# Six pairs of a triangular inverse merged in one pass, and norm weights loaded first

## The chip, the cores and the metric

The kernel runs on one core of a Trainium2 chip. The metric is the device time of one execution in microseconds (us). Engine names are those of the profile: PE is the matmul engine TensorE, DVE is VectorE, ACT is ScalarE, POOL is GpSimd, SP is SyncE, whose queue issues nearly all transfers.

## The reference

One layer of a decoder trunk: 256 tokens of width 2048, 256 memory tokens. The token mixer is a gated DeltaNet with 24 value heads of width 128 (two heads share one key and query head, which makes 12 pairs). Beside it runs a cross-attention with 4 heads. Both read columns of one input projection; the result is gated by SiLU and goes through one output projection.

The part that the change touches is the chunked delta rule. For each head and chunk a unit lower triangular system is solved:

```python
kk = jnp.einsum("bhncd,bhnjd->bhncj", k, k)
m = jnp.where(strict, beta[..., :, None] * kk * decay, 0.0) + jnp.eye(C, dtype=f32)
rhs = jnp.concatenate([v * beta[..., None], k * (beta * jnp.exp(gc))[..., None]], axis=-1)
sol = lax.linalg.triangular_solve(m, rhs, left_side=True, lower=True, unit_diagonal=True)
```

The kernel uses chunks of 128 tokens, so it has 12 pairs x 2 heads x 2 chunks = 48 matrices of 128x128 to invert, four to a pair.

## The kernel before

**Main stream.** Weights come in 275 tiles of 512 KB. SP issues their loads into five buffers `st`; ACT rounds each to `wt` (the high part) and DVE subtracts to get the low part; PE multiplies. Two forms of stream products exist: `pa` (a 512-column and a 256-column product for each of 16 blocks) and `pb` (three 512-column products for each block). `PLAN` is the list of weight tiles in the order in which they are used: memory values and keys, gates, cross-attention queries, key tiles, SiLU gates (`Z`), query and value tiles, output projection (`o`).

**What sets the order.** The kernel is written by a planner. It keeps an estimate `now` of the time on PE, advanced by `mm` for each product, and estimates of when ACT and DVE are free. Work beside the stream is written as generators that say with `yield` how long to wait, and with `until` on what; `step_side` runs those that are due between two stream products. `pe_soon` waits until the copies issued so far should be done. Instructions issued before `now` = 45 us, or put through `keep_in_program_order`, stay in the written order; the rest is ordered by a scheduler with times of its own, so a written run of small products can be cut by stream products. Every engine executes its own queue strictly in order: an instruction that waits holds all behind it.

**Start.** `first_loads` issues on ACT's queue the first half of the first memory tile `mst`, then the small table `prm` (norm weights), then the second half. `mem_prep` on DVE multiplies `mst` by a column of `prm` into `mkt`, high and low part; a stream product needs `mkt` and `wt`. `WARM` small products on zeros run before. In `gates`, an ACT instruction reads `prm` into `nA`, and a DVE instruction reads `nA`.

**Inverse.** Pairs 0 to 5 are group 0, pairs 6 to 11 are group 1. `inverse(g)` waits for the six pairs' matrices (`gram`), gets the 32x32 diagonal blocks through DRAM, inverts them on DVE column by column, and writes them to DRAM in two layouts, `dX` (natural) and `dY` (transposed). Then, for each two pairs (three times in a group), POOL clears `XN` and two `Y`, SP issues 6 transfers into `XN` and 8 into `Y`, and `merge` puts the blocks together:

```python
for s_ in range(4):
    for e, f in ef:
        mm(a1[at(e, f), s_, :], n2[e][f + 32 : f + 64, s_, f : f + 32], ys[e][f + 32 : f + 64, s_, f + 32 : f + 64],
           start=True, stop=True)
yield 0.2
se.copy(a, a1)
yield from pe_soon()
```

Four such runs follow each other, each needing the copies of the one before: 16 products of 32x32 (`pm<-Y,dec`), 24 of 32x32 (`pm<-Am,XN` and `pm<-XN,Am`), 8 of 64x64 (`pm<-Y,dec`) and 8 of 64x64 (`pm<-A,XN`). ACT copies the results back (`Am`, `XN`, `Y`, `A`). One fp32 product is two records of the trace. The result `Y` of a pair is what `delta` multiplies with.

**Delta.** `delta(p)` runs for pairs 0 to 11 in order (`pkq`, `pvt`, `pU`, `pO`, `pqs` products), each after the pair's `Y`, its value tiles and the delta before. `split_y` transposes its result (`pyT`) for the output projection, whose last weight tile of each column block needs pair 11.

Of the kernel before, what the change touches and what calls it, by code (L numbers as in the profile page):

```python
# [21 lines left out]
NB = 2  # L22
# [9 lines left out]


LOOK = 2
WARM = 7
XPACE = 3.0
HOP = 0.25
PINNED = 45.0
SLACK = 0.7
POLL = 0.3  # L40
CALM = 1.6
INV_CALM = 1.2
GATE_CALM = 1.6
LATE_DECAY = ("q", 3)
# [37 lines left out]
def hybrid_kernel(ctx: ExitStack, tc: tile.TileContext, x, xT, memT, W, prm_d, cst_d, out):  # L82
# [3 lines left out]
    def pin(ins):  # L86

        return tc.keep_in_program_order(ins) if PINNED is None or now[0] < PINNED else ins
# [57 lines left out]
    cp = ctx.enter_context(tc.tile_pool(name="cp", bufs=1))  # L146
    stp = ctx.enter_context(tc.tile_pool(name="stp", bufs=5))
    wp = ctx.enter_context(tc.tile_pool(name="wp", bufs=4))
    s2p = ctx.enter_context(tc.tile_pool(name="s2p", bufs=66))
    smp = ctx.enter_context(tc.tile_pool(name="smp", bufs=3))  # L150
    ps = ctx.enter_context(tc.tile_pool(name="ps", bufs=1, space=PSUM))
    dp = ctx.enter_context(tc.tile_pool(name="dp", bufs=1, space=DRAM))
# [1 line left out]
    def S2(name, shape, dt=F32):  # L154
        return s2p.tile([128] + list(shape), dt, name=name, tag="s2")

    def SM(name, shape, bufs=3, dt=F32):
        n = 1
        for d in shape:
            n *= d  # L160
        if n > 128:
            return smp.tile([128] + list(shape), dt, name=name, tag="s1k", bufs=12)
        if n > 16:
            return smp.tile([128] + list(shape), dt, name=name, tag="s512", bufs=3)
        return smp.tile([128] + list(shape), dt, name=name, tag=name, bufs=bufs)
# [20 lines left out]
    def bank(tag, name):  # L186
        yield from until(lambda: spare(tag))
        return PS(tag, name)
# [8 lines left out]
    def mm(o_, lhsT, rhs, start, stop):  # L197
        n = width(rhs)
        if rhs.dtype == F32:
            now[0] += {32: 0.015, 64: 0.038}.get(rhs.shape[0], max(0.19, 4 * n / 2400.0))  # L200
        else:
            now[0] += max(0.092, n / 2400.0 + 0.017)
        te.matmul(o_, lhsT, rhs, start=start, stop=stop)
# [96 lines left out]

    def first_loads():

        mst[0] = S2("mst", [512])
        for a in range(2):
            w = slice(a * 256, (a + 1) * 256)
            pin(nc.scalar.dma_start(mst[0][:, w], memT[0][:, w]))
            if a == 0:
                pin(nc.scalar.dma_start(prm[:, 0:P_CW], prm_d[:, 0:P_CW]))

    def wnext():  # L310
        while wpos[0] < len(PLAN) and free:
# [303 lines left out]
    def gates(pt):  # L615
# [14 lines left out]
        ve.tensor_scalar(out=gn[rbeta], in0=ab[rbeta], scalar1=-1.0, scalar2=80.0, op0=ALU.mult, op1=ALU.min)  # L630
        ve.scalar_tensor_tensor(out=gn[ra], in0=gx[ra], scalar=-1.0, in1=gx[ra], op0=ALU.mult, op1=ALU.min)
        yield
        se.activation(nA[ra, 0:1], prm[ra, P_AL : P_AL + 1], AF.Exp)
        se.activation(gu[ra], gn[ra], AF.Exp)
        se.activation(gu[rbeta], gn[rbeta], AF.Exp)
        yield
# [256 lines left out]
    def inverse(g):  # L893
        yield from until(lambda: all(p in grams for p in range(6 * g, 6 * g + 6)))
        yield 0.5
        nn = [S2("inN", [16, 32])[0:96] for _ in range(2)]
        xt = [S2("inXT", [16, 32])[0:96] for _ in range(2)]
        for f in range(2):
            sd.dma_start(nn[f], diag(dN[g])[:, 16 * f : 16 * f + 16])
        for f in range(2):  # L900
            po.memset(xt[f], 0.0)
        yield
        for f in range(2):
            po.memset(xt[f].rearrange("s c r -> s (c r)")[:, 16 * f : 512 : 33], 1.0)
        yield
        for i in range(1, 32):
            yield from calm(INV_CALM)
            work = []
            for f in range(2):
                w, j0 = min(16, i - 16 * f), 16 * f  # L910
                if w > 0:
                    tm = S2("inT", [16 * 32])[0:96]
                    work.append((f, w, j0, tm[:, 0 : w * (i - j0)].rearrange("s (c j) -> s c j", c=w)))
            for f, w, j0, tv in work:
                ve.tensor_tensor(out=tv, in0=xt[f][:, 0:w, j0:i],
                                 in1=nn[i // 16][:, i % 16, j0:i].unsqueeze(1).to_broadcast([96, w, i - j0]), op=ALU.mult)
            for f, w, j0, tv in work:
                ve.tensor_reduce(out=xt[f][:, 0:w, i], in_=tv, axis=AX.X, op=ALU.add)
            if len(work) == 1:
                ve.run(0.25)  # L920
        yield
        xn = nn
        for f in range(2):
            for e in range(2):
                ve.tensor_copy(xn[e][:, :, 16 * f : 16 * f + 16], xt[f][:, :, 16 * e : 16 * e + 16].rearrange("s c r -> s r c"))
        yield
        for f in range(2):
            sd.dma_start(dY[g][:, 16 * f : 16 * f + 16], xt[f])
        for f in range(2):
            sd.dma_start(dX[g][:, 16 * f : 16 * f + 16], xn[f])  # L930
        yield
        nat = dX[g].rearrange("(s k) r c -> k r s c", k=4)
        tsp = dY[g].rearrange("(s k) r c -> k r s c", k=4)
        for q in range(3):
            xs = S2("XN", [8, 64])
            ys = [S2("Y", [4, C]) for _ in range(2)]
            for t in [xs] + ys:
                po.memset(t, 0.0)
            yield
            for e in range(2):  # L940
                for k, r0, c0 in ((0, 64 * e, 0), (1, 64 * e + 32, 32), (2, 96 - 64 * e, 0)):
                    sd.dma_start(xs[r0 : r0 + 32, 4 * e : 4 * e + 4, c0 : c0 + 32],
                                 nat[k][:, 8 * q + 4 * e : 8 * q + 4 * e + 4])
            for p2 in range(2):
                s0 = 8 * q + 4 * p2
                for k in range(4):
                    b = slice(32 * k, 32 * k + 32)
                    sd.dma_start(ys[p2][b, :, b], tsp[k][:, s0 : s0 + 4])
            yield
            yield from merge(6 * g + 2 * q, xs, ys)  # L950

    def merge(p0, xs, ys):

        n2 = [N2[p0 + e].rearrange("r b h c -> r (b h) c") for e in range(2)]
        ef = [(e, f) for e in range(2) for f in (0, 64)]

        def at(e, f):

            r = 64 * e if f == 0 else 96 - 64 * e
            return slice(r, r + 32)

        pm = yield from bank("m", "pm")
        a1, y12, x21 = [pm[:, w * 128 : w * 128 + 128].rearrange("r (s c) -> r s c", s=4) for w in range(3)]
        a = SM("Am", [4, 32])
        for s_ in range(4):
            for e, f in ef:
                mm(a1[at(e, f), s_, :], n2[e][f + 32 : f + 64, s_, f : f + 32], ys[e][f + 32 : f + 64, s_, f + 32 : f + 64],
                   start=True, stop=True)  # L970
        yield 0.2
        se.copy(a, a1)
        yield from pe_soon()
        for s_ in range(4):
            for e, f in ef:
                r = at(e, f)
                mm(y12[r, s_, :], xs[r, 4 * e + s_, 0:32], a[r, s_, :], start=True, stop=True)
            for e in range(2):
                r = at(e, 0)
                mm(x21[r, s_, :], a[r, s_, :], xs[r, 4 * e + s_, 0:32], start=True, stop=True)  # L980
        yield 0.2
        for e in range(2):
            se.copy(xs[64 * e + 32 : 64 * e + 64, 4 * e : 4 * e + 4, 0:32], x21[at(e, 0)])
        for e, f in ef:
            se.copy(ys[e][f : f + 32, :, f + 32 : f + 64], y12[at(e, f)])
        give(pm, se.end)
        yield from pe_soon()
        pm2 = yield from bank("m", "pm2")
        a2, yab = [pm2[:, w * 256 : w * 256 + 256].rearrange("r (s c) -> r s c", s=4) for w in range(2)]
        A2 = SM("A2", [4, 64])  # L990
        for s_ in range(4):
            for e in range(2):
                mm(a2[64 * e : 64 * e + 64, s_, :], n2[e][64:128, s_, 0:64], ys[e][64:128, s_, 64:128], start=True, stop=True)
        yield 0.2
        se.copy(A2, a2)
        yield from pe_soon()
        for s_ in range(4):
            for e in range(2):
                r = slice(64 * e, 64 * e + 64)
                mm(yab[r, s_, :], xs[r, 4 * e + s_, :], A2[r, s_, :], start=True, stop=True)  # L1000
        yield 0.2
        for e in range(2):
            se.copy(ys[e][0:64, :, 64:128], yab[64 * e : 64 * e + 64])
        give(pm2, se.end)
        yield from pe_soon()
        for e in range(2):
            Y[p0 + e], N2[p0 + e] = ys[e].rearrange("r (b h) c -> r b h c", b=NB), None


    yhi, ylo = [None] * 16, [None] * 16  # L1010
# [75 lines left out]
    def delta(p):  # L1086
# [61 lines left out]
        yield from pe_soon()  # L1148
        for h in range(2):
            mm(B[:, 256 + h * C : 256 + (h + 1) * C], y[:, 1, h, :], vs[:, 1, h, :], start=True, stop=True)  # L1150
        A = yield from bank("A", "pO1")
        exact(A[:, 256:512], (kch[:, 1, :], kcl[:, 1, :]), (uh, ul), start=True, stop=True)
        yield 0.2
# [83 lines left out]
    first_loads()  # L1237
    spawn(mem_stats(), 8.0)
    spawn(tok_prep(), 8.0)
    spawn(inverse(0))  # L1240
    spawn(inverse(1))
    for hd in range(4):
# [90 lines left out]
```

## Time and profile before

| | |
|---|---|
| median of 3 runs | 879.3 us (878.26 to 879.44) |
| profiled execution | 878.1 us, span of its instructions 876.3 us |
| PE busy | 866.8 us, 99% |
| DVE, ACT, POOL busy | 639.4 us (73%), 539.8 us (62%), 45.5 us (5%) |
| HBM read | 158.14 MB, 188 GB/s over the span |

The profile gives for each instruction its engine, start and duration, and infers what ended the idle time before it. `pa<-hkt,wt` reads: products that write `pa` from the operands `hkt` and `wt`. A matmul's end is modelled and overlaps the next one's start, so the cost of one in a stream is read from the distance of starts, not from its duration.

### The profile page before, as it was taken

How to read it: one execution, taken by the hardware profiler on the slowest of the kernel's cores; microseconds unless marked ns; L12 is line 12 of the kernel's file. 1: busy time of each engine (PE TensorE's matmuls, PEld its weight loads, DVE VectorE, ACT ScalarE, POOL GpSimd, SP SyncE). 2: the span in 40 equal slices, each digit the busy share in tenths (PEclk: the TensorE clock that was granted, in tenths of full speed). 3: DMA queues.
4: the chain of work that ended last, by engine and by line, in shares of the span. 5: the costliest groups of instructions: out<-in, count | busy, mean ns of one | idle time of the engine just before them, and what ended most of it. 6: DMA issues, size and time to landing. Idle time of an engine off the chain costs nothing.

```text
span 876.3 us, 13987 instructions
## 1 busy us (share of the span) xinstructions
PE 866.8 (99%) x5091; PEld 731.9 (84%) x5091; DVE 639.4 (73%) x1277; ACT 539.8 (62%) x938; POOL 45.5 (5%) x62
## 2 busy tenths in 40 slices
PE   8999999999999999999999999999999999999998
PEld 5888889888888888788888888888888888888886
DVE  7778898578787998668789997554878855454542
ACT  7655665668776655665489866765677654333331
POOL 0000001000000000101000121100000000000000
PEclk9999999999999999999999999999999999999999
DMA  9865554467788756545765556444534546766660
GB/s 348 304 215 180 165 190 128 154 205 222 234 247 244 236 196 195 186 119 169 227 201 186 169 169 190 127 144 154 164 126 144 170 167 226 229 198 213 205 203 25
DMA packets 98638, 165.91 MB, mean 189 GB/s; under 512 B 24304, under 2 KB 64008, under 8 KB 98568
## 3 DMA queue, kind: packets, MB, share of 16 engines
q1 hardware_dynamic: 98136, 164.72, 58.8%
q8 instruction: 40, 0.66, 0.3%
q10 hardware_dynamic: 432, 0.28, 0.1%
q14 instruction: 30, 0.25, 0.1%
HBM read 158.14 MB, written 6.84 MB: 188 GB/s over the span
## 4 chain that ended last, share of the span: by engine, by line
PE 97%; ACT 1%; DMA 0%; issue 0%; DVE 0%; SPq 0%; DVEq 0%; ACTq 0%
PE pb L95 50%; PE pa L95 36%; PE pO L95 2%; PE pm L95 2%; PE pkq L95 1%; PE pU L95 1%; PE pyT L95 1%; PE xsc L95 1%; PE xo L95 1%; PE pkk L95 1%; PE pvt L95 1%; PE pqs L95 0%; DMA st<-W_d 0%; PE pab L95 0%; ACT Y L112 0%
## 5 line engine op out<-in xcount | busy, mean ns | idle before, releaser
L330 DVE TENSOR_TENSOR wt<-st,wt 128x1024 fp32r<-128x1024 f32 (+1 forms) x274 | 333.6, 1218 | 132.4 <-ACT wt L326 130.6
L326 ACT CAST wt<-st 128x1024 fp32r<-128x1024 f32 (+1 forms) x274 | 286.3, 1046 | 176.4 <-PE pb L95 134.7
L95 PE MATMUL pa<-hkt,wt 128*128 128x512 f32 (+1 forms) x1792 | 338.8, 343 | 1.2 <-ACT zs L112 1.2
L95 PEld LDWEIGHTS pa<-hkt,wt 128*128 128x128 f32 x1792 | 274.4, 189 | 39.6 <-ACT zs L112 1.7
L95 PE MATMUL pb<-wt,hkt 128*128 128x512 f32 x768 | 182.0, 393 | 0.0
L95 PEld LDWEIGHTS pb<-wt,hkt 128*128 128x128 f32 x768 | 141.8, 188 | 28.6
L95 PE MATMUL pb<-wt,yhi 128*128 128x512 f32 x512 | 158.5, 391 | 0.0
L95 PEld LDWEIGHTS pb<-wt,yhi 128*128 128x128 f32 x512 | 95.3, 188 | 19.3
L95 PE MATMUL pb<-wt,ylo 128*128 128x512 f32 x256 | 99.8, 390 | 0.0
L95 PE MATMUL pb<-wt,mkt 128*128 128x512 f32 x384 | 90.6, 396 | 2.5 <-DVE mkt L112 2.2
L95 PEld LDWEIGHTS pb<-wt,mkt 128*128 128x128 f32 x384 | 72.5, 191 | 19.0 <-ACT nA L112 3.1
L112 DVE SCALAR_TENSOR_TENSOR acc<-raw,prm,acc 128x255 f32<-128x255 f32 x144 | 69.0, 479 | 4.6 <-ACT acc L112 3.4
L112 ACT COPY raw<-pa 128x512 f32<-128x512 f32 x56 | 32.7, 585 | 53.2 <-PE pa L95 53.1
L95 PEld LDWEIGHTS pb<-wt,ylo 128*128 128x128 f32 x256 | 48.1, 188 | 10.1
L112 ACT ACT_TABLE_LOAD x33 | 42.3, 1283 | 2.2 <-DVE acc L112 1.6
L112 DVE TENSOR_TENSOR raw<-raw 128x256 f32<-128x256 f32 x57 | 23.9, 420 | 17.0 <-ACT raw L112 16.1
L112 POOL TENSOR_TENSOR e<-e,mhalf 128x4 f32<-128x4 f32 x12 | 16.5, 1372 | 302.7 <-DVE e L112 279.0
L112 DVE TENSOR_TENSOR inT<-inXT,inN 96x1 f32<-96x1 f32 (+22 forms) x92 | 29.5, 342 | 0.5
L112 DVE TENSOR_REDUCE inXT<-inT 96x1 f32<-96x1 f32 (+22 forms) x92 | 28.7, 337 | 0.7
L112 ACT ACTIVATE acc<-raw,prm 128x256 f32<-128x256 f32 x48 | 24.4, 508 | 4.3 <-DVE raw L112 4.2
L112 DVE TENSOR_SCALAR dec<-erow,gcc 128x128 f32<-128x128 f32 x96 | 23.9, 281 | 4.3 <-DMA erow<-dgc 4.3
L112 DVE SCALAR_TENSOR_TENSOR o<-o,e,zs 128x128 f32<-128x128 f32 x48 | 14.3, 348 | 12.3 <-POOL e L112 12.2
(197 smaller groups left out, 687.8 us busy)
## 6 DMA issues: line engine op xcount, KB each, us to landing
st<-W_d SPq DMA_DIRECT2D x272, 512.0 KB, 4.0
erow<-dgc SPq DMA_DIRECT2D x24, 256.0 KB, 5.2
dN<-dec SPq DMA_DIRECT2D x12, 256.0 KB, 3.0
xraw<-xT_d SPq DMA_DIRECT2D x8, 256.0 KB, 5.5
res<-x_d SPq DMA_DIRECT2D x8, 256.0 KB, 5.0
mst<-memT_d SPq DMA_DIRECT2D x7, 256.0 KB, 6.0
out_dram<-res SPq DMA_DIRECT2D x7, 256.0 KB, 4.8
inN<-dN SPq DMA_DIRECT2D x4, 192.0 KB, 5.0
```

The costliest lines, as they stand in the source:

```text
L95: return lambda *a, **k: pin(getattr(self.eng, op)(*a, **k))
L112: return pin(getattr(self.eng, op)(*a, **k))
L326: pin(se.eng.copy(hi[:, w] if parts > 1 else hi, st[:, w] if parts > 1 else src))
L330: pin(ve.eng.tensor_tensor(out=lo[:, w] if parts > 1 else lo, in0=st[:, w] if parts > 1 else src, in1=hi[:, w] if parts > 1 else hi, op=AL ...
```

## The change

`inverse` now makes one merge for the six pairs of a group. `Y` and `XN` become two tiles of the whole program (`yall`, `xall`), cleared once by a generator `blank`, whose three POOL instructions stand at the start of POOL's queue. Per group SP issues 4 transfers into `Y` (768 rows of 128 bytes each) and 6 into `XN` (384 rows each), 20 in the program where there were 84 of 128 rows each. `merge` is written in four runs of 48, 72, 24 and 24 products, eight in the program where there were 24 runs; the products are the same 336. The copies get three times as wide, or as wide and twice as many (384 columns). Since there is one `Y`, group 1 waits until `delta(5)` has read it. In `first_loads`, `prm` goes first; the ACT instruction that makes `nA` is kept where it is written, in `gates`; `WARM` goes from 7 to 8; two pools get smaller.

```diff
-WARM = 7
+WARM = 8
+LAND = 6.0
-    s2p = ctx.enter_context(tc.tile_pool(name="s2p", bufs=66))
+    s2p = ctx.enter_context(tc.tile_pool(name="s2p", bufs=60))
     def first_loads():
+        pin(nc.scalar.dma_start(prm[:, 0:P_CW], prm_d[:, 0:P_CW]))
         mst[0] = S2("mst", [512])
         for a in range(2):
             w = slice(a * 256, (a + 1) * 256)
             pin(nc.scalar.dma_start(mst[0][:, w], memT[0][:, w]))
-            if a == 0:
-                pin(nc.scalar.dma_start(prm[:, 0:P_CW], prm_d[:, 0:P_CW]))
...
-        se.activation(nA[ra, 0:1], prm[ra, P_AL : P_AL + 1], AF.Exp)
+        tc.keep_in_program_order(se.activation(nA[ra, 0:1], prm[ra, P_AL : P_AL + 1], AF.Exp))
...
+        yield from until(lambda: g == 0 or "y5" in ready)
         nat = dX[g].rearrange("(s k) r c -> k r s c", k=4)
         tsp = dY[g].rearrange("(s k) r c -> k r s c", k=4)
-        for q in range(3):
-            xs = S2("XN", [8, 64])
-            ys = [S2("Y", [4, C]) for _ in range(2)]
-            for t in [xs] + ys:
-                po.memset(t, 0.0)
...
+        for k in range(4):
+            b = slice(32 * k, 32 * k + 32)
+            sd.dma_start(yall[b, :, b], tsp[k])
+        for e in range(2):
+            for k, r0, c0 in ((0, 64 * e, 0), (1, 64 * e + 32, 32), (2, 96 - 64 * e, 0)):
+                sd.dma_start(xall[r0 : r0 + 32, e, :, c0 : c0 + 32], nat[k][:, 12 * e : 12 * e + 12])
+        yield LAND
+        yield from merge(g)
...
+        (pm,) = yield from banks(1)
+        a1, a = part(pm, 32), S2("Am", [12, 32])
+        for s_ in range(12):
             for e, f in ef:
-                mm(a1[at(e, f), s_, :], n2[e][f + 32 : f + 64, s_, f : f + 32], ys[e][f + 32 : f + 64, s_, f + 32 : f + 64],
+                mm(a1[at(e, f), s_, :], nt(e, s_)[f + 32 : f + 64, f : f + 32], yall[f + 32 : f + 64, 12 * e + s_, f + 32 : f + 64],
                    start=True, stop=True)
         yield 0.2
         se.copy(a, a1)
+        give(pm, se.end)
+        yield from pe_soon()
+        pms = yield from banks(2)
...
+        ready.add(f"y{p}")
...
+    spawn(blank(), 100.0)
```

**PE, first merge of group 0.** Its queue before, from the first small product of the first two pairs to the run of 24 (stream products `pa` between the runs are left out):

```order
L95 MATMUL pm<-Y,dec 32x32
...
L95 MATMUL pm<-Y,dec 32x32
...
L95 MATMUL pm<-Y,dec 32x32
...
L95 MATMUL pm<-Y,dec 32x32 x13
L95 MATMUL pa<-hkt,wt 128x256
L95 MATMUL pa<-hkt,wt 128x512
L95 MATMUL pa<-hkt,wt 128x256
L95 MATMUL pm<-Am,XN 32x32 x4
L95 MATMUL pm<-XN,Am 32x32 x2
```

And now, the same place for all six pairs:

```order
L96 MATMUL pm<-Y,dec 32x32
...
L96 MATMUL pm<-Y,dec 32x32 x47
L96 MATMUL pa<-hkt,wt 128x512
L96 MATMUL pa<-hkt,wt 128x256
L96 MATMUL pa<-hkt,wt 128x512
L96 MATMUL pa<-hkt,wt 128x256
L96 MATMUL pm<-Am,XN 32x32
L96 MATMUL pm<-XN,Am 32x32
...
L96 MATMUL pm<-Am,XN 32x32 x45
```

The written runs are cut by stream products in both, but less often now: over the whole queue the products `pm` stand in 39 uninterrupted runs before, in 16 now (10 in group 0, 6 in group 1).

**SP, the transfers of group 0.** Before, behind the last write of the blocks to DRAM (`st` are weight tiles; 4 and 5 weight tiles later the same 14 transfers come again for the next two pairs):

```order
L95 DMA dX_106<-inN 96x512
L95 DMA st<-W_d 128x1024 x3
L95 DMA XN<-dX_106 32x4x32 x6
L95 DMA Y<-dY_104 32x4x32 x8
L95 DMA st<-W_d 128x1024 x2
```

And now:

```order
L96 DMA dX_107<-inN 96x512
L96 DMA Y<-dY_105 32x24x32
L96 DMA st<-W_d 128x1024 x2
L96 DMA Y<-dY_105 32x24x32 x3
L96 DMA XN<-dX_107 32x12x32 x6
L96 DMA st<-W_d 128x1024 x3
```

All transfers of the group stand now where those of its first two pairs stood, one weight tile earlier.

**ACT, the end of the SiLU gate tile 4** (the last six `pb` products before query and value tiles go on). Before, with `kch` reading a product of `delta(5)`:

```order
L112 CAST kch<-pkq 128x256
L112 ACT_TABLE_LOAD
L112 ACTIVATE zs<-pb_5138 128x512
L112 ACTIVATE vs<-pvt,sV 128x128 x4
```

And now:

```order
L326 CAST wt<-st 128x1024
L113 ACT_TABLE_LOAD
L113 ACTIVATE zs<-pb_5047 128x512
L113 COPY u_5307<-pO_5253 128x256
L113 ACTIVATE oq<-pO_5291,egc 128x128 x2
```

The delta products that fall on this place are others, and the table load and `zs` no longer stand behind `kch`.

## Rows read from the trace of the kernel before

**Rows 1.** The page: busy time of the engines, share of the span, instructions.

```profile
PE 866.8 (99%) x5091; PEld 731.9 (84%) x5091; DVE 639.4 (73%) x1277; ACT 539.8 (62%) x938; POOL 45.5 (5%) x62
```

**Rows 2.** Chain of waits: shares, then pieces of stream (start, duration, what).

```profile
PE 97%; ACT 1%; DMA 0%; issue 0%; DVE 0%; SPq 0%; DVEq 0%; ACTq 0%
...
423.72 26.13 PE pa L95 x148
...
732.34 140.15 PE pb L95 x618
```

**Rows 3.** Timeline of PE from 575 us: start, duration, operation, records.

```profile
575.16 3.12 PE L95 MATMUL pb<-wt,hkt 128*128 128x512 f32 x13
578.21 0.45 PE L95 MATMUL pm<-Y,dec 32*32 32x32 f32 x32
578.59 0.97 PE L95 MATMUL pb<-wt,hkt 128*128 128x512 f32 x3
579.40 0.28 PE L95 MATMUL pU<-uh,kch 128*128 128x256 f32 x1
...
581.68 0.26 PE L95 MATMUL pm<-Am,XN 32*32 32x32 f32 x8
...
582.32 0.50 PE L95 MATMUL pb<-wt,hkt 128*128 128x512 f32 x1
```

**Rows 4.** Timeline of PE at 384 us, a run of one product.

```profile
384.84 0.24 PE L95 MATMUL pm<-Y,dec 32*32 32x32 f32 x2
385.01 1.32 PE L95 MATMUL pa<-hkt,wt 128*128 128x256 f32 x6
```

**Rows 5.** Timeline of PE at 589 us, a run of 64x64 products.

```profile
589.17 0.68 PE L95 MATMUL pm<-A,XN 64*64 64x64 f32 x16
589.78 1.66 PE L95 MATMUL pb<-wt,hkt 128*128 128x512 f32 x6
```

**Rows 6.** A group of PE, 344.8 to 392.5 us: records, busy, mean ns, idle before.

```profile
L95 PE MATMUL pm<-Y,dec 64*64 64x64 f32 x48 | 2.7, 226 | 0.5 <-ACT Y L112 0.4
```

**Rows 7.** Instructions on the tile `pm`: ACT copies, ns min/median/max.

```profile
L112 ACT COPY Am<-pm x6: 259/265/267, 349.5 to 578.7; 128x128 f32<-128x128 f32 x6
L112 ACT COPY A<-pm x6: 363/372/388, 353.3 to 587.1; 128x256 f32<-128x256 f32 x6
```

**Rows 8.** Timeline of ACT and PE at 505 us.

```profile
504.84 0.37 ACT L112 CAST kch<-pkq 128x256 fp32r<-128x256 f32 x1 [1.29 <-PE pkq L95]
505.23 1.28 ACT L112 ACT_TABLE_LOAD   x1
...
507.17 1.20 PE L95 MATMUL pa<-hkt,wt 128*128 128x512 f32 x5 [1.23 <-ACT zs L112]
```

**Rows 9.** Timeline of the first 17 us.

```profile
1.22 3.17 PE L95 MATMUL warm<-warm 128*128 128x512 bf16 x7 [1.22 <-DVE warm L112]
...
6.01 0.14 DVE L112 TENSOR_SCALAR nA<-nA 24x1 f32<-24x1 f32 x1 [4.85 <-ACT nA L112]
6.10 0.35 DVE L112 TENSOR_SCALAR mkt<-mst,prm 128x256 fp32r<-128x256 f32 x1
...
7.23 0.63 ACT L112 ACTIVATE msq<-mst 128x512 f32<-128x512 f32 x1 [1.25 <-DMA mst<-memT_d]
...
7.63 8.63 PE L95 MATMUL pb<-wt,mkt 128*128 128x512 f32 x31 [0.26 <-DVE wt L330]
```

**Rows 10.** DMA issues: KB each, median us to landing.

```profile
inN<-dN SPq DMA_DIRECT2D x4, 192.0 KB, 5.0
...
mst<-memT_d ACTq DMA_DIRECT2D x2, 128.0 KB, 3.9
...
prm<-prm_d ACTq DMA_DIRECT2D x1, 20.0 KB, 4.3
```

**Rows 11.** Timeline of SP's queue, group 0.

```profile
338.78 2.78 SPq L95 DMA_DIRECT2D XN<-dX  x6
341.65 4.61 SPq L95 DMA_DIRECT2D Y<-dY  x8
```

**Rows 12.** Engines from 592 to 720 us: length, PE, PEld, DVE, ACT, POOL busy, clock, DMA.

```profile
592.00:720.00 128.00, 128.00 (x756) 112.07 (x755) 92.87 (x163) 85.33 (x185) 4.03 (x4) 1.00 0.47 153
```

More of the change, by code (lines that the diff above doesn't have):

```diff
@@ L161, in SM @@
         if n > 128:
[L162 removed]
+            return smp.tile([128] + list(shape), dt, name=name, tag="s1k", bufs=10)
         if n > 16:
@@ L931, in inverse, with blank, merge, nt @@
         yield
+        yield from until(lambda: g == 0 or "y5" in ready)
         nat = dX[g].rearrange("(s k) r c -> k r s c", k=4)
         tsp = dY[g].rearrange("(s k) r c -> k r s c", k=4)
-        for q in range(3):
-            xs = S2("XN", [8, 64])
-            ys = [S2("Y", [4, C]) for _ in range(2)]
-            for t in [xs] + ys:
-                po.memset(t, 0.0)
[L939 to L956, printed above, removed]
+        for k in range(4):
[6 more added lines that the diff above has]
+        yield from merge(g)
+    yall = cp.tile([128, 24 * C], F32, name="Y", tag="Y").rearrange("r (s c) -> r s c", c=C)
+    xall = cp.tile([128, 24 * 64], F32, name="XN", tag="XN").rearrange("r (e s c) -> r e s c", e=2, c=64)
+    def blank():
+        for e in range(2):
+            po.memset(yall[:, 12 * e : 12 * e + 12, :], 0.0)
+            yield 5.0
+        po.memset(xall, 0.0)
+    def merge(g):
+        n2 = [[N2[6 * g + 3 * e + i].rearrange("r b h c -> r (b h) c") for i in range(3)] for e in range(2)]
         ef = [(e, f) for e in range(2) for f in (0, 64)]
+        def nt(e, s_):
+            return n2[e][s_ // 4][:, s_ % 4, :]
         def at(e, f):
@@ L962, in at, with banks, part @@
             return slice(r, r + 32)
[L964 to L967, printed above, removed]
+        def banks(n):
+            yield from until(lambda: spare("m", n))
+            return [PS("m", "pm") for _ in range(n)]
+        def part(pt, c):
+            return pt[:, 0 : 12 * 32].rearrange("r (s c) -> r s c", c=c)
+        (pm,) = yield from banks(1)
+        a1, a = part(pm, 32), S2("Am", [12, 32])
+        for s_ in range(12):
             for e, f in ef:
-                mm(a1[at(e, f), s_, :], n2[e][f + 32 : f + 64, s_, f : f + 32], ys[e][f + 32 : f + 64, s_, f + 32 : f + 64],
+                mm(a1[at(e, f), s_, :], nt(e, s_)[f + 32 : f + 64, f : f + 32], yall[f + 32 : f + 64, 12 * e + s_, f + 32 : f + 64],
                    start=True, stop=True)
@@ L972, in merge @@
         se.copy(a, a1)
+        give(pm, se.end)
         yield from pe_soon()
-        for s_ in range(4):
+        pms = yield from banks(2)
+        y12, x21 = [part(t, 32) for t in pms]
+        for s_ in range(12):
             for e, f in ef:
                 r = at(e, f)
-                mm(y12[r, s_, :], xs[r, 4 * e + s_, 0:32], a[r, s_, :], start=True, stop=True)
+                mm(y12[r, s_, :], xall[r, e, s_, 0:32], a[r, s_, :], start=True, stop=True)
             for e in range(2):
@@ L979, in merge @@
                 r = at(e, 0)
-                mm(x21[r, s_, :], a[r, s_, :], xs[r, 4 * e + s_, 0:32], start=True, stop=True)
+                mm(x21[r, s_, :], a[r, s_, :], xall[r, e, s_, 0:32], start=True, stop=True)
         yield 0.2
         for e in range(2):
-            se.copy(xs[64 * e + 32 : 64 * e + 64, 4 * e : 4 * e + 4, 0:32], x21[at(e, 0)])
+            se.copy(xall[64 * e + 32 : 64 * e + 64, e, :, 0:32], x21[at(e, 0)])
+        give(pms[1], se.end)
         for e, f in ef:
-            se.copy(ys[e][f : f + 32, :, f + 32 : f + 64], y12[at(e, f)])
@@ L986, in merge @@
-        give(pm, se.end)
+            se.copy(yall[f : f + 32, 12 * e : 12 * e + 12, f + 32 : f + 64], y12[at(e, f)])
+        give(pms[0], se.end)
         yield from pe_soon()
[L988 to L991, printed above, removed]
+        pms = yield from banks(2)
+        A2 = [S2("A2", [6, 64]) for _ in range(2)]
+        for s_ in range(12):
@@ L992, in merge @@
             for e in range(2):
-                mm(a2[64 * e : 64 * e + 64, s_, :], n2[e][64:128, s_, 0:64], ys[e][64:128, s_, 64:128], start=True, stop=True)
+                mm(part(pms[s_ // 6], 64)[64 * e : 64 * e + 64, s_ % 6, :], nt(e, s_)[64:128, 0:64],
+                   yall[64:128, 12 * e + s_, 64:128], start=True, stop=True)
         yield 0.2
-        se.copy(A2, a2)
+        for i in range(2):
+            se.copy(A2[i], part(pms[i], 64))
+            give(pms[i], se.end)
         yield from pe_soon()
-        for s_ in range(4):
+        pms = yield from banks(2)
@@ L998, in merge @@
+        for s_ in range(12):
             for e in range(2):
                 r = slice(64 * e, 64 * e + 64)
-                mm(yab[r, s_, :], xs[r, 4 * e + s_, :], A2[r, s_, :], start=True, stop=True)
+                mm(part(pms[s_ // 6], 64)[r, s_ % 6, :], xall[r, e, s_, :], A2[s_ // 6][r, s_ % 6, :], start=True, stop=True)
         yield 0.2
-        for e in range(2):
-            se.copy(ys[e][0:64, :, 64:128], yab[64 * e : 64 * e + 64])
-        give(pm2, se.end)
+        for i in range(2):
+            for e in range(2):
+                s0 = 12 * e + 6 * i
+                se.copy(yall[0:64, s0 : s0 + 6, 64:128], part(pms[i], 64)[64 * e : 64 * e + 64])
+            give(pms[i], se.end)
@@ L1005, in merge @@
         yield from pe_soon()
-        for e in range(2):
-            Y[p0 + e], N2[p0 + e] = ys[e].rearrange("r (b h) c -> r b h c", b=NB), None
+        for p in range(6):
+            Y[6 * g + p], N2[6 * g + p] = yall[:, 4 * p : 4 * p + 4, :].rearrange("r (b h) c -> r b h c", b=NB), None
     yhi, ylo = [None] * 16, [None] * 16
```

## The prediction, made before the changed kernel ran

> **What bounds the kernel now.** I read the page first: PE is busy for 866.8 of 876.3 us, and no other engine is near that [rows 1]. Then the chain of waits: 97% of it is PE [rows 2]. So the end comes when PE has worked through its queue, and a change counts by what it takes out of that queue or adds as a wait at its head. Third, the timeline of PE, for what one thing in the queue costs. A stream of `pb` takes 140.15 us for 618 products, 0.227 each; `pa` takes 26.13 us for 148, or 0.353 for a pair of 512 and 256 columns [rows 2]. What disturbs a stream is read against these steps.
>
> **The change part by part.**
>
> *The runs of small products, the main term.* Take the run at 578.21 [rows 3], 16 products (32 records). The 13 `pb` before it take 578.21 - 575.16 = 3.05 us, where 13 steps are 2.95: going in costs 0.10. The run itself lasts until the next stream product starts, 0.38. The 3 `pb` behind it take 0.81 where 3 steps are 0.68: coming back costs 0.13. Together 0.61. Now a run of one product [rows 4]: 0.17 to the next start, which with the same 0.23 around it is 0.40. So 15 more products cost 0.21, 0.014 each, and the rest, about 0.38, is paid per run. The run of 24 lasts 0.64 [rows 3] and the eight of 64x64 last 0.61 [rows 5]; both have the same edges around them, so they differ only by what they hold.
>
> The products are the same 336 before and after, only the number of runs falls: from the 39 that stand in PE's queue to 16, not from 24 to 8 as written. I take 0.37 for a run, a little under 0.38, since a run beside other small products shares an edge: 23 x 0.37 = **8.5 us less**. Bounds: the middle alone, without edges, is 23 x 0.16 = 3.7; the highest price with a wait in front that also goes, 0.45, gives 10.4.
>
> *Waits inside a merge.* In the stage of group 0 PE stood idle 0.5 us before the 64x64 products, mostly for the ACT copies of `Y` [rows 6]. There are fewer such places now, but each has longer copies in front: 0.27 us for 128 columns, 0.37 for 256 [rows 7], so by the same step about 0.48 for 384. Behind the 47 products four stream products stand, 0.7 us, before the first of the next run; the copy and about 0.25 us until the products have drained and the copy has begun fill just that. Six copies follow the second run, some 2.4 us, where the order leaves 1.8 to 1.9 us of stream in either group before the first 64x64 product, which needs the fourth or fifth of them at the latest. I put **0.2 more** than before on this; bounds: none, and 0.5 at each of the 8 stages, 4 us.
>
> *The end of a gate tile.* At 505.94 PE stops for 1.23 us because the next accumulator is still to be read by `zs`. In ACT's queue `zs` and its table load (1.28) stand behind `kch`, which itself waited for a product of the delta [rows 8]. Now the table load stands behind a weight cast and ahead of the end of that accumulator, and between that end and the first `pa` PE has six `pb` and five delta products, about 2 us, for one `zs` of 0.6. **1.2 us less**; bounds 0 (another wait takes its place) and 1.23.
>
> *The start.* The first DVE work of weight, `mkt` at 6.10, stood behind `nA` at 6.01, which waited on ACT [rows 9]; `nA` now goes to `gates`. `mkt` then waits for `prm` and the first half of `mst`. On ACT's queue, issued at 0.73 and 1.17, they land some 4.3 and 3.9 us later [rows 10], so around 5.1, one microsecond sooner. But the second `mkt` needs the second half of `mst`, which is still the third transfer. ACT's square, which reads both halves, waited for it until 7.23 [rows 9], and the second `mkt` ran at 7.49. Only 0.26 us can be had there if that half lands as before. The other thing is the clock: the warm-up products run in (3.17 - 0.63)/6, or 0.42 each, 512 columns at the lower of the two levels of 1.2 and 2.4 GHz, and the first 31 `pb` take 8.63 us where 31 steps are 7.03 [rows 9, 2]. One warm-up product more and a first product 0.7 sooner leave a gap of about 1 us where it was 2.2, so the higher level may come earlier. **0.5 less**; bounds 0 and 1.6. `prm` and `mst` pass only each other; SP's queue is untouched there.
>
> *What costs nothing.* POOL's 18 clears of 512 columns become 3 of 1536 at the very start, when POOL has nothing else. ACT has 26 copies instead of 60 in the merges. SP's 84 transfers took 2.78 us for 6 and 4.61 for 8 [rows 11], during which no weight tile was issued; PE did not starve, because five tiles of `st` at 8 pairs each are 5 x 2.8 = 14 us of stream. Now SP has 10 in a row of about the same 0.45, so weights are held up less, not more. If that cover is gone, each tile that comes late stops PE for up to 2.8 us.
>
> *The new wait on SP.* In group 1 the four `Y` transfers wait until `delta(5)` has read `Y`. Behind them on SP are weight tiles, with the same 14 us of cover; the first product of the merge stands about 5 us of stream behind that read, the 47 others about 10. The transfers are 3072 rows of 128 bytes. Two transfers of 1536 such rows (`inN`) land 5.0 us after issue [rows 10]; 128-row transfers go at 768 in 2.78 us, 277 rows per us [rows 11]. Between about 800 per us (3072 in 5.5 us less a landing delay of 1.7) and 277, I take the faster, as 768 rows are nearer to 1536 than to 128: 3.8 + 1.7 = 5.5 us, in time for the 47.
>
> **The sum**, against the profiled execution: -8.5 + 0.2 - 1.2 - 0.5 = -10.0, so its 878.1 becomes 868.1. The median of the runs shown is 1.2 above that execution, so I forecast **869 us**, 1.2% faster.
>
> **A rule weighed against the rows.** The run at 578.21 puts 32 records on PE in 0.38 us, 12 ns each [rows 3]. The Trainium skill, "TensorE: Matmul & The Clock Gate", section "Wait — 56ns, not 53.3ns?", says that starts never come closer than about 25 ns, however few columns. By that rule the 672 records would take 16.8 us in either kernel, most of what the 39 runs cost in all, and the price per run would be nearer 0.18, the gain 23 x 0.18 = 4.2, the time 873.5. The row is twice as fast as the rule allows, for products that sit on different parts of the array, so I give this 2%.
>
> **The rivals.**
>
> 1. *Waits eat a part.* Each of the 16 runs finds its copies or transfers 0.25 us late, or the six late deltas lose 0.6 us each: +4, 873 us. For it: the copies are longer, and group 1's deltas start 20 us of stream later than before and follow each other closer. Against it: DVE and ACT are busy 73% and 67% from 592 to 720 us [rows 12], and the row of waits is short [rows 6]. 12%.
>
> 2. *Transfers at the small rate.* At 277 rows per us, group 0's last 4608 rows, issued from about 336, end near 355 with their landing, where PE wants them near 351.5; group 1's `Y` takes 11.1 + 1.7 against 11.3 us of PE until the 47. That is 3.5 + 1.5, and 874 us. Against it: the large transfers. 7%.
>
> 3. *Slower: PE stands before the merge.* The same place, a lower rate r: PE waits 4608/r - 13 in group 0 and 3072/r - 9.6 in group 1. The gain is gone at 7680/r = 32.6, r = 236 rows per us; at 200 the waits are 15.8 and the time 885. For it: weight tiles move beside the rows. Against it: even the small transfers beat 236 [rows 11]. 4%.
>
> 4. *Nothing is left of it.* The time given back by PE is lost at the end, because pair 11 comes late: its last product stands 2.7 us of stream later than before, and its transposes leave 4.2 us before the last weight tile of the first output block needs them. If six deltas each take 1.5 us longer than planned, PE waits there for what it saved, and the time is 878 to 880. DVE at 73% speaks against it. 7%.
>
> That the change merges less than it says is already in the 16.
>
> **How the numbers follow.** My forecast, 867 to 871.5, has 68%; the rule 2%; the rivals 12, 7, 4 and 7%. A measurement of this kernel tells about 0.2%, 1.8 us, from no change. Faster is 68 + 2 + 12 + 7 = 89%, the same 7%, slower 4%. The range goes from 865.5 (merge at 10.4 and start at 1.6 instead of 8.5 and 0.5, with a little waited elsewhere) to 874, with rivals 1 and 2 in it; nothing of rivals 3 and 4 is.
>
> **What would show it.** Products `pm` in 16 runs, none of them over 0.3 us idle before; a run of 45 or 47 in about 1 us; no idle of PE near 505; first `mkt` near 5.2 and first stream product near 5.8; SP's ten transfers in about 5 us, landing within 6. It is wrong if PE shows idle time before `pm<-Y,dec` with a DMA as releaser, if the deltas of pairs 6 to 11 show idle PE before `pU` or `pO`, or if the runs cost what they cost before in proportion to their products.

## The result, and the profile after

| | before | after |
|---|---|---|
| median | 879.1 us (878.26 to 879.44, 4 runs) | 868.5 us (867.75 to 869.76, 4 runs) |
| ratio, 95% interval | | 0.988 (0.987 to 0.990) |
| profiled execution, span | 878.1, 876.3 us | 867.8, 866.0 us |

1.2% faster, 10.3 us in the profiled executions. The page of the changed kernel first: PE is as full as in [rows 1] and [rows 2], only for a shorter time.

```profile
PE 860.1 (99%) x5092; PEld 729.3 (84%) x5092; DVE 638.8 (74%) x1277; ACT 536.2 (62%) x904; POOL 39.5 (5%) x47
...
PE 99%; DMA 1%; DVE 0%; ACTq 0%; issue 0%; DVEq 0%
```

**The runs.** PE's timeline of the changed kernel, group 0, then pieces of group 1 (start, duration, operation, records):

```profile
342.80 1.90 PE L96 MATMUL pa<-hkt,wt 128*128 128x512 f32 x10
344.63 0.24 PE L96 MATMUL pm<-Y,dec 32*32 32x32 f32 x2
344.80 2.70 PE L96 MATMUL pa<-hkt,wt 128*128 128x512 f32 x14
347.43 1.00 PE L96 MATMUL pm<-Y,dec 32*32 32x32 f32 x94
348.37 0.96 PE L96 MATMUL pa<-hkt,wt 128*128 128x512 f32 x4
349.26 0.24 PE L96 MATMUL pm<-Am,XN 32*32 32x32 f32 x2
...
355.28 1.17 PE L96 MATMUL pm<-Am,XN 32*32 32x32 f32 x90
356.38 2.13 PE L96 MATMUL pa<-hkt,wt 128*128 128x256 f32 x11
358.44 0.32 PE L96 MATMUL pm<-Y,dec 64*64 64x64 f32 x2
...
570.27 0.32 PE L96 MATMUL pm<-Y,dec 64*64 64x64 f32 x2
570.53 0.73 PE L96 MATMUL pb<-wt,hkt 128*128 128x512 f32 x2
571.25 1.61 PE L96 MATMUL pm<-Y,dec 64*64 64x64 f32 x46
572.79 1.43 PE L96 MATMUL pb<-wt,hkt 128*128 128x512 f32 x5
```

These answer to [rows 3 to 5]. A run of one product still takes 0.17 us to the next start (344.63 to 344.80). A run of 47 takes 0.94 (347.43 to 348.37), so 46 more products cost 0.77, 0.017 each. For 64x64 products, 23 take 1.54 (571.25 to 572.79) where one takes 0.26, so 0.058 each. If each run is charged with what it pushes the stream back (from the start of the last stream product ahead to the end of the first behind, less the steps of these two), the 39 runs of before cost 25.7 us and the 16 of after 16.4, **9.3 less**.

**The waits.** The view of waits for PE, from 20 us to the end, groups its idle time by what ended it (us in total, times, longest). Before:

```profile
PE pa L95 <- ACT zs L112: 1.2, 1, 1.2
PE pm L95 <- ACT Y L112: 0.6, 3, 0.2
```

In the changed kernel this view has no row at all: the wait for `zs` [rows 8] and those for the copies of `Y` [rows 6] are gone, and no new one stands before a small product, a delta product or a transposition. Its timeline at the end of the gate tile (those rows of ACT, PE and PE's weight loads, PEld, that bear on it):

```profile
496.43 1.28 ACT L113 ACT_TABLE_LOAD   x1
...
496.86 0.60 PE L96 MATMUL pO<-vs,Y 128*128 128x128 f32 x4
...
497.66 0.86 PE L96 MATMUL pb<-wt,hkt 128*128 128x512 f32 x3
497.72 0.60 ACT L113 ACTIVATE zs<-pb 128x512 f32<-128x512 f32 x1
...
498.37 1.71 PEld L96 LDWEIGHTS pa<-hkt,wt 128*128 128x128 f32 x10 [0.28 <-ACT zs L113]
498.37 2.03 PE L96 MATMUL pa<-hkt,wt 128*128 128x512 f32 x10
```

The table load is over at 497.71, `zs` at 498.32, and PE goes on to `pa` at 498.37 without a gap. The weight load of this `pa` still waits for `zs`, so `zs` comes just in time and nothing is left over.

**The copies**, wider now (ns min, median, max), where [rows 7] had 265 and 372 for 128 and 256 columns:

```profile
L113 ACT COPY Y<-pm x16: 468/472/478, 356.5 to 576.6; 32x384 f32<-32x384 f32 x8, 64x384 f32<-64x384 f32 x8
L113 ACT COPY Am<-pm x2: 481/482/482, 348.5 to 565.8; 128x384 f32<-128x384 f32 x2
```

**The start**, against [rows 9]:

```profile
1.21 3.59 PE L96 MATMUL warm<-warm 128*128 128x512 bf16 x8 [1.21 <-DVE warm L113]
...
4.81 0.35 DVE L113 TENSOR_SCALAR mkt<-mst,prm 128x256 fp32r<-128x256 f32 x1 [3.65 <-DMA mst<-memT_d]
...
5.31 0.76 PE L96 MATMUL pb<-wt,mkt 128*128 128x512 f32 x1 [0.50 <-DVE mkt L113]
...
6.53 0.35 DVE L113 TENSOR_SCALAR mkt<-mst,prm 128x256 fp32r<-128x256 f32 x1 [0.25 <-DMA mst<-memT_d]
```

The first stream product starts at 5.31 instead of 6.60. But the thirteenth is only 0.6 us earlier, and at 320 us, ahead of the merges, the lead is only 0.12. It is still 0.6 at 78 us; what takes the rest between 107 and 143 us is not shown.

**SP**, group 0 (against [rows 11]), and the landing of the group's transfers (window from 332 to 345 us; KB each, median us from issue to landing):

```profile
332.83 0.37 SPq L96 DMA_DIRECT2D Y<-dY  x1
333.94 2.41 SPq L96 DMA_DIRECT2D st<-W_d  x2
336.40 2.19 SPq L96 DMA_DIRECT2D Y<-dY  x3
338.70 5.49 SPq L96 DMA_DIRECT2D XN<-dX  x6
...
Y<-dY SPq DMA_DIRECT2D x4, 96.0 KB, 6.4
XN<-dX SPq DMA_DIRECT2D x6, 48.0 KB, 2.4
```

### The profile page after: what moved, and what is told of

It reads as the page before. It is cut to its first block, busy times and chain, and to the rows that moved or that the text cites. A ratio compares the mean times of both kernels' runs of the same rounds, so it can differ in the third digit from the quotient of the medians.

```text
span 866.0 us, 13821 instructions
## 1 busy us (share of the span) xinstructions
PE 860.1 (99%) x5092; PEld 729.3 (84%) x5092; DVE 638.8 (74%) x1277; ACT 536.2 (62%) x904; POOL 39.5 (5%) x47
## 4 chain that ended last, share of the span: by engine, by line
PE 99%; DMA 1%; DVE 0%; ACTq 0%; issue 0%; DVEq 0%
PE pb L96 51%; PE pa L96 37%; PE pO L96 2%; PE pm L96 2%; PE pkq L96 1%; PE pU L96 1%; PE pyT L96 1%; PE xsc L96 1%; PE xo L96 1%; PE pkk L96 1%; PE pvt L96 1%; DMA mst<-memT_d 1%; PE pqs L96 0%; PE pab L96 0%; PE xpT L96 0%; PE pk L96 0%
## 5 line engine op out<-in xcount | busy, mean ns | idle before, releaser
L96 PE MATMUL pa<-hkt,wt 128*128 128x512 f32 (+1 forms) x1792 | 334.6, 341 | 0.0
L113 ACT ACTIVATE dec<-dec 128x512 f32<-128x512 f32 x24 | 15.2, 631 | 12.8 <-DVE dec L113 12.6
```

What stands on the lines that cost most here:

```text
L96: return lambda *a, **k: pin(getattr(self.eng, op)(*a, **k))
L113: return pin(getattr(self.eng, op)(*a, **k))
```

## The experiments

The theory: the gain is the fixed price of a run, paid 23 times less, and the wait for `zs`. The rivals: the gain is in the transfers (20 instead of 84); it is in the waits for copies; it is in the start. Times are medians; ratios are to the kernel before, run beside each.

| kernel | us | ratio (95%) |
|---|---|---|
| before, start edits only | 879.3 | 1.000 (0.999 to 1.001) |
| changed, without the start edits | 870.0 | 0.990 (0.988 to 0.991) |
| changed, runs whole | 869.6 | 0.989 (0.988 to 0.990) |
| changed, each small product twice | 895.9 | 1.020 (1.018 to 1.022) |
| before, runs whole | 881.8 | 1.003 (1.002 to 1.004) |
| changed, small transfers | 871.3 | 0.991 (0.990 to 0.992) |
| before, SiLU first | 878.8 | 1.000 (0.999 to 1.001) |
| changed, runs whole, other warm-up | 873.1 | 0.993 (0.992 to 0.995) |
| changed, other warm-up | 871.2 | 0.990 (0.989 to 0.992) |
| changed, once more | 869.6 | 0.989 (0.987 to 0.990) |

### 1 and 2. The start alone, the merge alone

The first is the kernel before with `prm` first, `nA` kept in `gates` and `WARM = 8`; the second is the changed kernel with these three taken back (a part of its edit):

```diff
-        pin(nc.scalar.dma_start(prm[:, 0:P_CW], prm_d[:, 0:P_CW]))
         mst[0] = S2("mst", [512])
...
+            if a == 0:
+                pin(nc.scalar.dma_start(prm[:, 0:P_CW], prm_d[:, 0:P_CW]))
```

> The kernel before with the three edits of the start alone (norm weights first on ACT's queue, the ACT instruction of nA kept in the gates, one warm-up product more); the merges stay as they were, 39 runs on PE. Theory (PE's queue sets the end; the start gave 0.57 us at the 13th stream product of the changed kernel, of which 0.12 were left at 170 us): 0.1 to 0.6 us faster than before, 878.5 to 879.0, first stream product near 5.3 us, and PE still idle about 1.2 us near 505 us for zs. Rival (the start carries most of the gain, since the earlier stream shifts everything): 3 us or more faster, under 876.

> The changed kernel with the three edits of the start undone. Theory: the merge alone carries the gain, 16 runs on PE instead of 39 at 0.37 to 0.40 us each, and no wait for zs: 9.9 to 10.6 us faster than before, 868.5 to 869.2, first stream product near 6.6 us. Rival (start carries most): within 3 us of before.

The start alone gave 879.28 us against 879.23, no change that can be measured, though its first stream product starts at 5.57, a microsecond sooner. The merge alone gave 870.0, a little over the 868.5 to 869.2 expected; it has the 16 runs, and no row of PE waiting for `zs`. With the start edits alone that wait is still there:

```profile
506.81 1.91 PE L95 MATMUL pa<-hkt,wt 128*128 128x512 f32 x9 [1.24 <-ACT zs L112]
```

So the merge carries the gain, the place of `zs` with it. With the start alone, the lead of 1.03 us at the first stream product is 0.27 at the thirteenth: the first products run at the lower clock, and by their steps it rises near 10.6 us, where before it rose near 10.3. How far the rise moves by itself is read from windows of the changed kernel and of its repetition (experiment 9): length, busy time and records of PE, PEld, DVE, ACT, POOL, then granted clock, DMA share, GB/s. The changed kernel:

```profile
9.50:11.00 1.50, 1.50 (x7) 1.22 (x6) 1.50 (x3) 1.50 (x5) 0.00 (x0) 1.00 1.04 415
11.00:13.00 2.00, 2.00 (x10) 1.68 (x9) 1.88 (x3) 2.00 (x4) 0.00 (x0) 1.00 1.02 410
```

The same program once more:

```profile
9.50:11.00 1.50, 1.50 (x5) 1.13 (x4) 1.50 (x3) 1.50 (x4) 0.00 (x0) 0.50 1.03 408
11.00:13.00 2.00, 2.00 (x9) 1.60 (x8) 1.94 (x4) 2.00 (x5) 0.00 (x0) 0.76 1.03 413
```

At the lower of the clock's two levels a `pb` takes 0.43 us instead of 0.23. The step changes for good at about 9.9 us in the one execution and at about 11.7 in the other, with the same program. (The clock column reads 1.00 for the changed kernel even before 9.9 us, where the steps are 0.43, so the time is read from the steps. In the repetition they were 0.23 once already, near 7.2 us, and fell back.) In other traces the step changed at 12 us and later. At 142 us the two executions of one program are 0.9 us apart, about as much as an earlier first product could give.

### 3. The runs kept whole

Small products, and the stream product behind each run, stay in the written order; 10 runs instead of 16:

```diff
-        te.matmul(o_, lhsT, rhs, start=start, stop=stop)
+        ins = te.matmul(o_, lhsT, rhs, start=start, stop=stop)
+        small = rhs.shape[0] in (32, 64)
+        if small or was_small[0]:
+            tc.keep_in_program_order(ins)
+        was_small[0] = small
...
```

> The changed kernel with its small products, and the stream product behind each run, kept in the written order on PE: 10 runs in the queue instead of 16. Theory (a price per run, 0.37): 6 x 0.37 = 2.2 us faster than the changed kernel, 866.3, unless PE now waits at the head of a run for its transfers or copies. Rival 1 (the price goes with the products, not the runs): same as the changed kernel, 868.5. Rival 2 (waits take its place): idle time of PE before pm of 2 us or more, 868.5 to 872.

No gain, as the second rival had it: 869.6 us, and the small products cost 16.5 us as in the 16 runs. Six runs fewer should be 2.2 us; two waits, 2.1 in sum, took them back, in its timeline of PE:

```profile
355.27 0.32 PE L96 MATMUL pm<-Y,dec 64*64 64x64 f32 x2
355.99 0.69 PE L96 MATMUL pm<-Y,dec 64*64 64x64 f32 x10 [0.40 <-ACT Y L113]
...
566.20 0.22 PE L96 MATMUL pm<-Am,XN 32*32 32x32 f32 x3 [1.69 <-issue]
```

The first is a copy that the stream products in a cut run hide. The second has no releaser and stands in the middle of a run of 72. Just ahead, at 563.73, one packet moves on the DMA queue of instructions (a window of 0.1 us there; packets, MB, share):

```profile
q8 instruction: 1, 0.02, 74.5%
```

Without these two waits the small products would cost 14.4 us, 2.0 less than in the 16 runs, or 0.33 for each of the six (an estimate). The second wait led to experiments 8 and 9.

### 4. Each small product twice

```diff
         te.matmul(o_, lhsT, rhs, start=start, stop=stop)
+        if rhs.shape[0] in (32, 64):
+            te.matmul(o_, lhsT, rhs, start=start, stop=stop)
```

> The changed kernel with each of the 336 small products issued twice in a row (the second writes the same numbers again); 14 runs on PE instead of 16. Theory (a product of 32x32 costs 0.014 to 0.021 us in a run, one of 64x64 0.055 to 0.058): 96 x 0.016 + 144 x 0.021 + 96 x 0.058 = 10.1 more, two runs less, 0.7: 868.5 + 9.4 = 878. Rival (25 ns for each of 672 more records): 16.8 more, 884.6. Rival (products are free, only runs count): 868.

The expectation missed the time by 18 us, though the term that it was to test held: 0.023 us for each 32x32 product added and 0.061 for each 64x64, where the clock was full. By these the 240 and 96 products of 336 would add 11.4 us. The median is 27.4 higher; the profiled execution, the slowest of the four, is 31.8 longer than that of the changed kernel. Of these 31.8, 6.2 are five waits inside runs with the releaser "issue", and much of the rest is the clock, in its windows (the number behind POOL's):

```profile
355.00:360.00 5.00, 3.65 (x182) 2.99 (x181) 0.01 (x1) 1.57 (x4) 0.00 (x0) 1.00 0.49 193
360.00:377.00 17.00, 16.10 (x220) 14.06 (x221) 5.04 (x12) 5.62 (x10) 0.70 (x1) 0.50 0.11 33
...
588.80:598.90 10.10, 8.79 (x293) 7.36 (x281) 0.00 (x0) 3.11 (x7) 0.00 (x0) 0.50 0.01 3
```

For 17 us after a stretch in which PE was busy 3.65 of 5 us, the granted clock is 0.50, the lower level, and again for 10 us in group 1. PE works 24.9 us in these two stretches, so half the clock costs some 12 (an estimate). With the products and the waits, less two runs, that is 29 of the 31.8.

### 5. The kernel before, runs kept whole

The edit of experiment 3, made in the kernel before; 31 runs instead of 39.

> The kernel before with its small products, and the stream product behind each run, kept in the written order on PE: 31 runs instead of 39, transfers and products as before. Theory (0.37 us per run of small products): 8 x 0.37 = 3.0 us less in the merges, 876.3, where no wait takes its place. Rival (the gain of the change came from the transfers or from fewer copies, not from the number of runs): as before, 879.

Wrong in sign: 881.8 us, slower. Its waits of PE:

```profile
PE pm L95 <- DMA Y<-dY: 2.6, 5, 0.8
PE pa L95 <- ACT zs L112: 1.2, 1, 1.2
```

Eight runs fewer should give 3.0 us, but now PE stands in front of transfers still on their way. In the kernel before, stream products stand between the products of the first run while the blocks of `Y` land one after the other: each cut pays the price of a run and hides a landing. Here, fewer runs can be had only where all data of a run have landed, which one large early batch of transfers does and this edit does not.

The waits alone, 2.6 us, would not make it slower. The rest is the granted clock, which falls to its lower level twice in group 0, each time shortly after such waits (windows as in experiment 4):

```profile
350.20:353.60 3.40, 3.40 (x57) 2.71 (x56) 0.00 (x0) 1.48 (x6) 0.00 (x0) 0.50 1.01 358
...
387.80:391.10 3.30, 3.30 (x12) 2.82 (x11) 2.09 (x7) 3.21 (x14) 1.01 (x1) 0.50 0.06 17
```

At half the clock these 6.7 us cost some 3.3 (an estimate). Eight runs less (-3.0), the waits for `Y` copies that went (-0.6), the new waits (+2.6) and the clock (+3.3) make +2.3; the profiled execution is 3.3 longer than that of the kernel before. The other executions agree: two of the twelve, with a mean granted clock of 0.998, took 877.0 and 879.1 us, the ten with 0.992 to 0.996 took 880.7 to 884.0.

### 6. The changed merge with small transfers

```diff
-            sd.dma_start(yall[b, :, b], tsp[k])
+            for s0 in range(0, 24, 4):
+                sd.dma_start(yall[b, s0 : s0 + 4, b], tsp[k][:, s0 : s0 + 4])
```

and the same for `XN`: 84 transfers of 128 rows, as before the change.

> The changed kernel with its transfers cut back to 84 of 128 rows, all of a group in a row on SP; 16 runs on PE as in the changed kernel. Theory (transfers lie beside PE): within 1 us of the changed kernel, 868 to 870, if the rows still land before their products; at 277 rows per us they land 3.5 us late in group 0 and 1.5 in group 1, then 873 with PE idle before pm. Rival (the smaller number of transfers carries the gain): 876 or more without such idle time.

871.3 us, over the 868 to 870 expected and 1.8 above the changed kernel on the same chip (experiment 9), still 7.8 below before. SP takes 12 us for 23 transfers, and PE waits:

```profile
PE pm L96 <- issue: 0.7, 1, 0.7
PE pm L96 <- DMA Y<-dY: 0.6, 1, 0.6
PE pm L96 <- DMA XN<-dX: 0.4, 1, 0.4
```

The 0.7 is a stop inside a run, of the kind seen in experiment 3. So the small transfers cost about 1 us here (0.6 + 0.4) of the gain, and the runs keep the rest. In the changed kernel the transfers of group 0 are in time: the last `Y` is issued at 337.4 and lands 6.4 us later, 0.8 ahead of the first small product (344.63) and 3.6 ahead of the run of 47. Of the six `XN` the trace has the landing of four; the fourth took 2.0 us, and if the last, issued at 343.7, takes as long, it lands near 345.7 (an estimate), 3.6 ahead of 349.26 where it is wanted.

### 7. SiLU first on ACT, in the kernel before

```diff
-            spawn(silu(pt, cb, r), 0.2)
+            g = silu(pt, cb, r)
+            next(g)
+            spawn(g, 1.0)
...
-        se.activation(zs[cb][r], pt, AF.Silu)
+        tc.keep_in_program_order(se.activation(zs[cb][r], pt, AF.Silu))
```

> The kernel before with the SiLU of a gate tile's accumulator written at once and kept in that order on ACT, so that it no longer stands behind kch. Theory: PE's idle 1.23 us near 505 us (for zs) goes, 1.2 us faster, 878.0. Rival: the time is given back at the next wait, as before, 879.2.

The wait for `zs` went, yet the time did not change: 878.8 us. The edit moved other work: there are 40 runs, the merges of group 0 end later, and PE waits 0.3 for a copy of `Y` in front of `pkk`. By the charge used above, its runs cost 26.0 us instead of 25.7. So some 0.6 of the 1.2 could be left, less than the interval of this ratio can tell from nothing. What the wait is worth alone stays open; that it is gone in the changed kernel is seen, not tested.

### 8 and 9. The same code at another place

The warm-up becomes 64 small products, in the kernel of experiment 3 and in the changed kernel, which moves all that follows on PE by 112 instructions. Beside the latter the changed kernel ran again.

```diff
-    for _ in range(WARM):
-        te.matmul(wps, warm[:, 0:128], warm, start=True, stop=True)
+    for _ in range(8 * WARM):
+        te.matmul(wps[0:32, 0:64], warm[:, 0:32], warm[:, 0:64], start=True, stop=True)
```

> The kernel with 10 whole runs, whose 8 warm-up products of 512 columns are now 64 of 64 columns: 112 more instructions on PE ahead of everything else, same order behind them. In the kernel with 10 whole runs PE stood idle 1.7 us inside the second run of group 1, with no releaser, 0.6 us after the code queue had begun to load its next 16 KB. Theory (PE ran out of instructions; where that happens depends on where the 16 KB blocks end): that wait goes or moves to another place, pm in all 1.5 to 2 us cheaper if no other appears, near 867.5. Rival (PE waited for a transfer or a copy there): the wait stays at the same product with the same length.

> The changed kernel with 64 warm-up products of 64 columns in place of 8 of 512, which moves every later instruction of PE by 112 places and does no other work. Theory A (PE sometimes runs out of instructions, and where that falls depends on the place of a run in the program): the waits with the releaser 'issue' inside the long runs of group 0 and 1 change, 0.5 to 3 us of them instead of 0.2, and the time is 869 to 872 us. Theory B (the 16 cut runs of the changed kernel never empty the queue, wherever they stand, since stream products between them give time to load): no such wait over 0.3 us, and 868.5 us, plus up to 0.5 for the different warm-up.

> The changed kernel once more, on the same chip as the run beside it. Both theories: 868.5 us (867.5 to 870), no wait with the releaser 'issue' over 0.2 us inside a run of small products, 16 runs.

In the kernel with whole runs the waits moved as the theory of instructions wants, but grew instead of going, so 867.5 us was missed with 873.1. A part of this is the clock: its six executions go from 871.0 us at a mean granted clock of 0.998 to 875.6 at 0.991. Its timeline has one where there was none, and a shorter one in group 1:

```profile
354.02 0.22 PE L96 MATMUL pm<-XN,Am 32*32 32x32 f32 x2 [2.78 <-issue]
...
568.64 0.22 PE L96 MATMUL pm<-Am,XN 32*32 32x32 f32 x3 [1.11 <-issue]
```

In the changed kernel with the other warm-up, the run of 72 products in group 1, which took 1.64 us to the next stream product, now stops (timeline of PE):

```profile
571.31 0.22 PE L96 MATMUL pm<-Am,XN 32*32 32x32 f32 x2 [1.28 <-issue]
```

The runs are the same 16 in the same order, and this one takes 1.5 us longer. The time is 871.2 us, 1.6 above the changed kernel beside it, but not all of that is the stop's: in the profiled executions the merges already begin 1.4 us later (346.9 and 345.5), and those of group 1 still 1.0 later (561.7 and 560.7), since the start is another. The two parts can't be told apart in the medians. The repetition has no such row; a gap of 0.3 us in one run is all.

Every such stop ends the same time after a load on the instruction queue has begun. For the eleven stops of 0.3 us and more, in five kernels and the repetition, that time is 2.25 to 2.60 us: the one above ends at 571.31, the load began at 568.96; in experiment 3, 566.20 and 563.73; in experiment 8, 354.02 and 351.58. A theory in which the cut runs are safe wherever they stand is thus wrong. What fits is that PE waits for instructions: where a load begins near the head of a long run, the run uses up those it has before the next have come. No view names this cause. In two of the eleven (experiments 4 and 8) PE stood about 0.5 us already when the load began; why it began so late is not shown.

## Why the prediction was right

The forecast was 869 us, the result 868.5; the sum was -10.0 against the profiled execution, which lost 10.3. By its steps:

- **Runs, -8.5.** Held. The price of 0.37 for a run is what a run of one product costs in the changed kernel too, and 16 runs were found. The 9.3 hold the waits in front of the 64x64 products: 0.6 us by the view of waits, 1.3 by what the four runs that had them cost over like runs without. That leaves 8.0 to 8.7, or 0.35 to 0.38 for each of the 23. No experiment changed the number of runs and nothing else, since in 3 and 5 waits came in; with these taken off, 3 gives 0.33 for a run. The Trainium skill, "TensorEngine Tiling (Array Packing)", "Key Properties", says that TensorE drains when it changes the tiling mode, not when it changes the tile; a fixed price for each run and little for a product agrees with that.
- **Waits inside a merge, +0.2.** Wrong in sign: -0.6 to -1.3, since the idle time in front of 64x64 products went and next to nothing came. The copies take 0.47 us as estimated; but six of them are 2.9 us, as found in group 1 (568.3 to 571.2), and not the 2.4 of the prediction. What the step did not see is that the order splits the third run: one product behind the copy that it needs, the other 23 about a microsecond later (358.44 and 359.47; 570.27 and 571.25), with stream products up to each. In ACT's timeline of group 1 the copies that they wait for end at 570.2 and 571.2:

```profile
569.75 1.45 ACT L113 COPY Y<-pm 32x384 f32<-32x384 f32 x3
```

- **The end of the gate tile, -1.2.** The wait is gone as read from ACT's order, though with nothing to spare.
- **The start, -0.5.** Mis-sized in both directions: `prm` and the first half of `mst` landed 3.1 and 3.5 us after their issue and not 4.3 and 3.9, so the first product came 1.3 earlier and not 0.7; yet 0.12 us is left at 320 us, and alone it can't be measured.
- **SP's ten transfers, about 5 us.** They took 11.4, of which 2.4 are weight tiles and 2.5 a pause after the first `XN`. In group 0 `Y` took 6.4 us to land and not 6 at most. It cost nothing, since the rows were there 0.8 us ahead of the first small product (experiment 6).

Added up, 9.3, 1.2 and 0.1 are 10.6; 0.3 of loss elsewhere is not placed. That the sum came within 0.3 us is in part luck: the waits came out 0.8 or more better than forecast, the start 0.4 worse. The lower end of the range, 865.5, is below what its own terms give (869 - 1.9 - 1.1 = 866.0); nothing hangs on it. Of the rivals, the one by the rule of 25 ns a start falls: 94 records in 0.94 us are 10 ns each, and the products of experiment 4 agree. Rivals 1 to 3 fall with the empty view of waits; experiment 6 shows that rival 2 was the nearest. Rival 4 falls too, since no delta and no transposition finds PE idle. A cost that no step had is the stop of PE inside a run, after a load on the instruction queue. The changed kernel nearly escapes it; with its code at another place one run of it took 1.5 us more.

## What to carry to other kernels

Where one engine is full, count how often it leaves its stream and not only how much it does there: here an excursion cost 0.37 us and a small product in it 0.02 to 0.06. Before holding such work together by order alone, look at what the interruptions hide; with data still on the way they turn into waits, as in experiment 5. Look at the granted clock after new waits: in experiment 5 it cost as much as the waits themselves. Long runs of very short instructions can stop, it seems for code, and a difference of 1 or 2 us between two versions may be the place of their code; shift the code to see.

## What the runs showed of the hardware

- PE seems to wait for its own instructions. They come in loads of 16 KB, with about 250 matmuls and weight loads between two of them in a stream; with 1344 more of these, experiment 4 has 45 loads where the changed kernel has 40. In runs with a small product every 16 to 60 ns PE stopped for 0.2 to 2.8 us, until 2.25 to 2.60 us after such a load began.
- Such a stop can cost more than itself. After the one of 2.78 us in experiment 8 the granted clock was 0.66 over the next 5 us, and 0.50 over 17 us in experiment 4; after those of 1.28 and 1.69 us it stayed at 1.00. The length of one stop does not decide it: in experiment 5 the clock fell to 0.50 after waits of 1.6 us in sum and again after 1.1, none of them over 0.83. Two windows of experiment 8:

```profile
351.00:355.00 4.00, 1.22 (x66) 1.02 (x55) 0.67 (x1) 0.33 (x1) 0.00 (x0) 1.00 0.94 340
355.00:360.00 5.00, 5.00 (x61) 4.10 (x59) 0.44 (x2) 4.07 (x9) 0.00 (x0) 0.66 0.02 8
```

- The time at which the clock rises at the start is not set by the program alone: it rose for good at 9.9 and 11.7 us in two executions of the same kernel.
